# A projection with its weights stationary and 512 tokens moving, and its result brought to its partitions through DRAM

## The chip, the cores and the metric

The kernel runs on one core of a Trainium2 chip. The time is the device time of one execution in microseconds. Before the change it was 2569.82 us, the median of three runs (2568.74 to 2572.65).

Five engines work side by side, each through its own instructions in order: TensorE (PE; the loads of its stationary operand are listed apart, as PEld), VectorE (DVE), ScalarE (ACT), GpSimd (POOL) and SyncE (SP), which issues most of the DMAs. An instruction that waits holds back everything behind it on its engine.

## The reference

Two model blocks are computed one after the other for 1024 tokens of 1024 channels, in float32. The change touches the S5 branch of the first block alone:

```
z = x @ w_in                                    # x: 1024 tokens x 1024
u_a, v_a, g_a, x_b, g_b, q_x, g_x = split(z)    # x_b: 256 channels
# S5: 16 groups of 16 channels, 64 complex states each
bu = einsum('gpc,blgc->blgp', b_bar, x_b)
h  = scan over the tokens: h[l] = lam_bar * h[l-1] + bu[l]
y  = gelu(real(einsum('gcp,blgp->blgc', c, h)) + d * x_b)
y_b = y * sigmoid(y @ glu_w + glu_b)            # then times silu(g_b)
```

The other branches of the first block are a gated spatial mixing (u_a, v_a, g_a) and an attention over a memory of 256 tokens (q_x, g_x). Then follow `w_out`, a layer norm, and the second block: a recurrent branch, a differential attention, a second memory attention, and 32 experts of which each token takes two.

## The kernel before

**Products.** Every large product is made of three matmuls on operands in two parts (high and low, float32r), by `mm3` (lines 172 to 176): left high with right high, left low with right high, left high with right low. The left operand is the stationary one, the right one moves. x lies transposed in `xh` and `xl`: 128 channels on the partitions, eight such tiles, 1024 tokens along the row.

**S5 in chunks.** The tokens are cut into 128 chunks of `CT` = 8. Within a chunk the outputs are a matrix times the inputs; the states go from chunk to chunk by a scan. The branch needs x_b in an unusual shape, for each group of 16 channels a tile with place and channel (8 x 16 = 128) on the partitions and the 128 chunks along the row. Before the change this took two steps:

- `inputs` (lines 541 to 554): for each of the 8 places a product with x stationary (128 tokens, one of every eight, so a column every 32 bytes) and the 256 columns of `w_xb` moving. Over 8 places, 8 channel tiles and 3 parts these are 192 matmuls into the PSUM tile `pu`. ACT copies them to `U`: chunks on the partitions, place and channel along the row.
- in `s5`, once for each of four units u of four groups (lines 604 to 609): four transposes on TensorE into the PSUM tile `px`, then the split into the two parts `X`.

After it each unit computes `pst` (what a chunk adds to the states), turns and scans it on DVE and POOL, makes the states `h`, and computes `py` from `h` and from `X` with the matrix `K`. After two units the outputs are transposed (`pty`), copied to `Y`, and at the end `pz` is the product with `glu_w`.

**What sets the order.** `inputs` is issued at a high priority, before three lanes that `merge` (lines 71 to 118) puts side by side by clocks of their own: `left` (S5, then half of the gating), `attend` (memory attention, tiles `pk`, `pv`, `pq`, `sc`, `pt`, `po`, then the other half of the gating, again into `pv`), and `dense`, products of 512 tokens into the tile `pj` that fill in. A scheduler then fixes each engine's order when the program is built. The pools have few buffers, and some tags are shared: `xraw` (the raw tiles of x), `U`, `K` and `yt` take turns in the buffers u0, u1, k and yt; the high and low parts of chunked weights have two buffers each, which `w_xb` fills until `inputs` is through and into which `xa_w_k` goes then.

Of the kernel before, what the change touches and what calls it, by code (L numbers as in the profile page):

```python
# [28 lines left out]
BLK = 96                    # tokens of a block of an expert  # L29
NB = -(-1024 // BLK)        # blocks that one expert can have  # L30
NY = 3
N0 = 2                          # gated outputs of the first branch that go under the attention
CT = 8                          # tokens of a chunk of the S5 states
NRA, NRB, NRX = 6, 6, 1                 # buffers of the expert weights
OVAT = 8                        # expert beside which the further blocks are listed
LIM = 78                        # chunks of expert weights after which fewer buffers take them
EMPTY = 2048                    # the token of an empty row, beyond all
NOV = 2048 // BLK + 1       # more than the blocks beyond the first ones
# [32 lines left out]
def merge(tc, lanes, fill, made):  # L71
    """emits the lanes side by side: each moves its own clock on by its pace with every step, and the one
    that is behind comes next; the clock is the priority too. A lane yields None, a new place for its
    clock, the name of work of the last lane that it needs, or a condition that another lane will fulfil.
    The last lane only has products that fill in; what takes them out of PSUM, the functions that it
    yields, goes first."""
# [3 lines left out]
    late = []  # L80
# [49 lines left out]
class Model:  # L130
# [50 lines left out]
    def gelu2(self, out, ps, pool, shape, tag):  # L181
        """out = 2 * gelu(ps)"""
        q = pool.tile(shape, F32, name=tag + "q", tag=tag + "q")
        self.act(q, ps, AF.Square, scale=GC0)
        self.stt(q, q, 1.0, ps, OP.add, OP.mult)
        self.act(q, q, AF.Tanh, scale=GC1)
        self.stt(out, q, 1.0, ps, OP.add, OP.mult)

    def exp_small(self, out, x, pool, w, name):
        """accurate exp of a small tile [128, w]"""  # L190
# [24 lines left out]
    def sincos(self, s, c, r, pool, shape, name):  # L215
        """r in [-pi, pi]"""
        a = pool.tile(shape, F32, name=name + "a")
        self.act(s, r, AF.Sin)
        self.ts(a, r, -1.0, OP.mult)
        self.tt(a, a, r, OP.max)  # L220
        self.ts(a, a, -1.0, OP.mult, math.pi / 2, OP.add)
        return self.act(c, a, AF.Sin)
# [14 lines left out]
    # ------------------------------------------------------------------  # L237
    def setup(self):
# [13 lines left out]
        # half biases for sigmoids made of tanh  # L252
# [4 lines left out]
        # residents that live into the second block  # L257
# [5 lines left out]
    def params(self, P):  # L263
        """S5 and rope tables, softplus of the LRU parameter, lambda of the differential attention;
        yields between its steps"""
# [8 lines left out]
        # S5: step, lambda * step  # L274
# [14 lines left out]
        # rotation of one step and of its doublings, up to half of all tokens  # L289
# [17 lines left out]
        # expm1(a) = 2 tanh(a/2) / (1 - tanh(a/2))  # L307
# [11 lines left out]
        # lambda to the powers 0 .. CT, and what a chunk leaves of a state's modulus  # L319
# [4 lines left out]
        for lev in range(4):  # L324
# [5 lines left out]
            if 0 < lev < 3:  # L330
                # the powers up to n times this one
# [11 lines left out]
        # f = (lambda_bar - 1) / lambda  # L343
# [13 lines left out]
        # b_bar = f * b  # L357
# [11 lines left out]
    def params2(self, P):  # L369
        nc, A = self.nc, self.A  # L370
        t = lambda k, w=8: P.tile([128, w], F32, name="par2_" + k)
        # rope angles
# [12 lines left out]
        # softplus(-lambda) of the LRU  # L385
# [19 lines left out]
        # lambda of the differential attention  # L405
# [11 lines left out]
    def s5_tables(self, x, y, tb, u):  # L417
        """cos(CT theta c), sin(CT theta c) of the chunks c, of two state tiles"""
# [16 lines left out]
        # ends with the last doubling  # L435

    # ------------------------------------------------------------------
    # first block
    # ------------------------------------------------------------------
# [12 lines left out]
    def block1(self):  # L452
# [29 lines left out]
        # x transposed, in two parts  # L482
# [13 lines left out]
        def group(ps, ws, h):  # L496
            """one product of 512 tokens, whole"""
# [27 lines left out]
        def store_y(k, t0, y, n):  # L525
            """n token tiles of channel tile k"""
# [3 lines left out]

        # ---- S5, in chunks of CT tokens: token CT c + t is place t of chunk c. Within a chunk the outputs
        # are a matrix times the inputs; the states go from chunk to chunk ----
        U = [S5.tile([128, 8, CT, 16], F32, name="U", tag=f"u{ct}") for ct in range(2)]
        # matrices with blocks of zeros that stay: states to outputs, inputs to states
# [6 lines left out]
        def inputs():  # L541
            """x_b with the chunks on the partitions; the places backwards"""
            for m in range(CT // 2):
                ps = PB.tile([128, 2, 256], F32, name="pu", tag="pb", bufs=2)
                for s in range(2):
                    t = 2 * m + 1 - s
                    for k in range(8):
                        w = w_xb[k // 4]
                        v = [z[:, k].rearrange("p (c t) -> p t c", t=CT)[:, t] for z in (xh, xl)]
                        self.mm3(ps[:, s], v, (w[0][:, k % 4], w[1][:, k % 4]), k == 0, k == 7)  # L550
                for ct in range(2):
                    j = CT - 2 - 2 * m
                    self.act(U[ct][:, :, j:j + 2].rearrange("p g j c -> p j g c"),
                             ps[:, :, 128 * ct:128 * ct + 128].rearrange("p s (g c) -> p s g c", c=16), AF.Copy)

        def s5():
            yield from self.params2(P)
            parp.__exit__(None, None, None)
            for u in range(4):
# [6 lines left out]
                def times(m, n, sign):  # L566
                    """m lambda^k, k < n; sign is that of the second part of m"""
# [13 lines left out]
                # states to outputs: c lambda^k  # L581
# [5 lines left out]
                # inputs to outputs: c lambda^k b, k < CT, with zeros before; every place's row is a window of it  # L587
# [16 lines left out]
                # inputs, places and channels on the partitions  # L604
                pb = PB.tile([128, 4, 128], F32, name="px", tag="pb", bufs=2)
                for g in range(4):
                    nc.tensor.transpose(pb[:, g], U[ct][:, 4 * (u % 2) + g].rearrange("p j c -> p (j c)"), self.ident)
                X = [S5.tile([128, 4, 128], F32R, name="xg", tag=f"xg{k}") for k in "hl"]
                self.split(X[0], X[1], pb)
                yield  # L610
                # what a chunk adds to the states
# [15 lines left out]
                # turned back, the states decay by a real factor  # L627
# [22 lines left out]
                # the states before each chunk  # L650
# [14 lines left out]
                # 2 gelu  # L665
# [12 lines left out]
                if u % 2:  # L678
                    # back to channels on the partitions
# [8 lines left out]
            # y_b = y * sigmoid(glu) * silu(g_b); y comes doubled  # L688
# [131 lines left out]
        def gating(hp, side, wload, vps, pm_):  # L820
            """two heads of the gating; wload loads weights, vps and pm_ say where in PSUM"""
# [1624 lines left out]
```

## Time and profile before

| | us |
|---|---|
| median of three runs | 2569.82 |
| span of the profiled execution, first to last instruction | 2566.8 |
| median less span (what lies around the span; the profile prints no time of its own for it) | 3.0 |
| TensorE busy in the span | 2402.1 |
| VectorE busy in the span | 1774.3 |
| `inputs`, starts of the first and the last matmul | 37.1 and 87.4 |
| start of the last `pty` of S5 | 304.1 |

A matmul's listed duration is not the time it adds: matmuls overlap, and where they follow one another without a gap the distance from start to start counts. Slices and stretches in which PE is busy throughout are those in which it had always something to do. The granted clock is 1 at 2.4 GHz and 0.5 at 1.2 GHz; a mean between the two says how much of a stretch had which.

### The profile page before, as it was taken

The page shows a single profiled execution, that of the slowest core. Times are in us where ns is not written, and L with a number is a line of the kernel's source. Part 1 is how long each engine was busy: PE and PEld are TensorE (multiplying, and loading weights), DVE is VectorE, ACT ScalarE, POOL GpSimd, SP SyncE. Part 2 cuts the span into 40 slices and gives each one's busy share as a digit, 9 for nine tenths or more (in the row PEclk, how much of TensorE's full clock was granted, in tenths as well). Part 3 has the DMA queues.
Part 4 walks back from the last instruction along what each step waited for, and adds up shares of the span by engine and source line. Part 5 has one row for each costly group of instructions (what it writes and reads, how often), then busy time and mean ns, then how long its engine had stood idle before and what let it go on. Part 6 is the DMA issues. An engine that isn't in the chain of part 4 may idle for free. (4 is left out here: it accounts for less than half of the span.)

```text
span 2566.8 us, 34716 instructions
## 1 busy us (share of the span) xinstructions
PE 2402.1 (94%) x13128; PEld 1993.8 (78%) x13128; DVE 1774.3 (69%) x3153; ACT 1246.6 (49%) x1854; POOL 595.1 (23%) x425
## 2 busy tenths in 40 slices
PE   6999989999999999999999989999998998999997
PEld 5988877777788889889898778888876776766665
DVE  8367576777796666666665654334557998998897
ACT  4234532344565445445445532124435776776665
POOL 4312212312222121121021010001222332233343
PEclk9999999999999999999999999999998999999999
DMA  4221245412221111101101256642246997999995
GB/s 167 63 73 63 81 140 173 134 68 78 72 85 46 50 42 54 54 30 54 61 35 40 92 193 211 200 154 91 83 197 243 366 379 284 331 372 359 353 341 200
DMA packets 101688, 392.18 MB, mean 153 GB/s; under 512 B 14352, under 2 KB 31248, under 8 KB 76944
## 3 DMA queue, kind: packets, MB, share of 16 engines
q1 hardware_dynamic: 82992, 333.31, 36.0%
q0 software_dynamic: 18528, 56.65, 7.0%
q8 instruction: 104, 1.70, 0.3%
q14 instruction: 64, 0.52, 0.1%
HBM read 338.02 MB, written 60.26 MB: 155 GB/s over the span
## 5 line engine op out<-in xcount | busy, mean ns | idle before, releaser
L154 ACT ACTIVATE wh<-raw 128x2048 fp32r<-128x2048 f32 (+2 forms) x310 | 480.0, 1557 | 322.4 <-PE pj L175 84.4
L166 DVE TENSOR_TENSOR wl<-raw,wh 128x2048 fp32r<-128x2048 f32 (+2 forms) x287 | 553.5, 1939 | 94.4 <-ACT wh L154 93.9
L174 PE MATMUL pj<-wh,xnh 128*128 128x256 f32 x768 | 222.9, 290 | 9.0 <-ACT pc L154 4.8
L2214 POOL DMA_INDIRECT out<-y,lsti x32 | 146.8, 4588 | 355.6 <-DVE y L162 351.2
L176 PE MATMUL pj<-wh,xnl 128*128 128x256 f32 x768 | 218.4, 284 | 0.0
L175 PE MATMUL pj<-wl,xnh 128*128 128x256 f32 x768 | 217.9, 284 | 0.0
L175 PE MATMUL pg<-wl,xh 128*96 128x512 f32 x512 | 205.1, 401 | 13.3 <-DVE wl L166 12.6
L176 PE MATMUL pg<-wh,xl 128*96 128x512 f32 x512 | 201.9, 395 | 0.0
L174 PE MATMUL pg<-wh,xh 128*96 128x512 f32 x512 | 200.5, 397 | 0.0
L174 PEld LDWEIGHTS pj<-wh,xnh 128*128 128x128 f32 x768 | 145.7, 190 | 11.9 <-ACT pc L154 6.7
L179 POOL TENSOR_TENSOR ss<-ss,mhalf 128x4 f32<-128x4 f32 (+1 forms) x68 | 74.3, 1093 | 315.5 <-DVE ss L163 223.5
L175 PEld LDWEIGHTS pj<-wl,xnh 128*128 128x128 f32 x768 | 146.6, 191 | 0.0
L176 PEld LDWEIGHTS pj<-wh,xnl 128*128 128x128 f32 x768 | 145.6, 190 | 0.0
L154 ACT ACTIVATE e<-sc,st,ss 128x1024 f32<-128x1024 f32 (+7 forms) x128 | 105.6, 828 | 67.8 <-DVE st L158 50.5
L175 PEld LDWEIGHTS pg<-wl,xh 128*96 128x96 f32 x512 | 82.8, 162 | 55.8 <-DVE wl L166 23.2
L174 PEld LDWEIGHTS pg<-wh,xh 128*96 128x96 f32 x512 | 83.0, 162 | 37.3 <-ACT wh L154 2.2
L176 PEld LDWEIGHTS pg<-wh,xl 128*96 128x96 f32 x512 | 83.2, 162 | 33.3 <-DVE xl L166 0.2
L174 PE MATMUL pj<-xnh,wh 128*128 128x512 f32 x256 | 103.3, 404 | 5.6 <-ACT wh L154 5.6
L174 PE MATMUL pg<-xnh,wh 128*128 128x512 f32 x256 | 103.7, 405 | 0.0
L175 PE MATMUL pg<-xnl,wh 128*128 128x512 f32 x256 | 102.6, 401 | 0.0
L176 PE MATMUL pg<-xnh,wl 128*128 128x512 f32 x256 | 102.4, 400 | 0.0
L175 PE MATMUL pj<-xnl,wh 128*128 128x512 f32 x256 | 102.2, 400 | 0.0
(1001 smaller groups left out, 6673.1 us busy)
## 6 DMA issues: line engine op xcount, KB each, us to landing
raw<-in_w_gu SPq DMA_DIRECT2D x128, 1024.0 KB, 8.7
raw<-in_w_dn SPq DMA_DIRECT2D x64, 1024.0 KB, 9.6
raw<-in_w_out SPq DMA_DIRECT2D x16, 512.0 KB, 4.0
ta<-tg POOLq DMA_DIRECT2D x32, 256.0 KB, 2.7
t<-ta SPq DMA_DIRECT2D x14, 512.0 KB, 4.7
raw<-in_w_ga SPq DMA_DIRECT2D x12, 512.0 KB, 3.7
raw<-in_w_v SPq DMA_DIRECT2D x12, 512.0 KB, 3.5
xraw<-in_xT SPq DMA_DIRECT2D x8, 512.0 KB, 6.9
```

The costliest lines, as they stand in the source:

```text
L154: return self.nc.scalar.activation(out=out, in_=in_, func=func, **kw)
L166: return (eng or self.nc.vector).tensor_tensor(out=out, in0=a, in1=b, op=op)
L174: mm(ps, l[0], r[0], start=start, stop=False)
L175: mm(ps, l[0], r[1], start=False, stop=False)
L176: mm(ps, l[1], r[0], start=False, stop=stop)
L179: self.nc.gpsimd.tensor_tensor(out=out, in0=in_, in1=self.mhalf[:, :w], op=OP.pow)
L2214: return nc.gpsimd.indirect_dma_start(out=self.out, out_offset=bass.IndirectOffsetOnAxis(ap=u["row"], axis=0), in_=u["y"], in_offset=None, ...
```

## The change

`inputs` now runs over two channel tiles ct and two halves h of the tokens. The 128 columns of `w_xb` are stationary and 512 neighbouring tokens move, as in `dense`: 2 x 2 x 8 x 3 = 96 matmuls of 512 columns. ACT copies each result into the tile `xbt` with places and chunks in another order. `xbt` is stored to DRAM (`xbd`, 512 KB for each ct), and eight DMAs for each ct (64 KB each, runs of 512 bytes) load it so that place and channel are on the partitions: `U` now has the shape that the transposes made. The 16 transposes are gone; `X` is split from `U` in SBUF. `xbt` takes the buffers k and yt.

```diff
-        U = [S5.tile([128, 8, CT, 16], F32, name="U", tag=f"u{ct}") for ct in range(2)]
+        U = [S5.tile([128, 8, 128], F32, name="U", tag=f"u{ct}") for ct in range(2)]
+        xbd = [D.tile([128, CT, 128], F32, name=f"xbd{ct}") for ct in range(2)]
...
-            for m in range(CT // 2):
-                ps = PB.tile([128, 2, 256], F32, name="pu", tag="pb", bufs=2)
-                for s in range(2):
-                    t = 2 * m + 1 - s
+            for ct in range(2):
+                xt = S5.tile([128, CT, 128], F32, name="xbt", tag=("k", "yt")[ct])
+                for h in range(2):
+                    ps = PB.tile([128, 512], F32, name="pu", tag="pb", bufs=2)
                     for k in range(8):
-                        w = w_xb[k // 4]
-                        v = [z[:, k].rearrange("p (c t) -> p t c", t=CT)[:, t] for z in (xh, xl)]
-                        self.mm3(ps[:, s], v, (w[0][:, k % 4], w[1][:, k % 4]), k == 0, k == 7)
-                for ct in range(2):
-                    j = CT - 2 - 2 * m
-                    self.act(U[ct][:, :, j:j + 2].rearrange("p g j c -> p j g c"),
-                             ps[:, :, 128 * ct:128 * ct + 128].rearrange("p s (g c) -> p s g c", c=16), AF.Copy)
+                        w = [z[:, k % 4, 128 * ct:128 * ct + 128] for z in w_xb[k // 4]]
+                        self.mm3(ps, w, (xh[:, k, hs(h)], xl[:, k, hs(h)]), k == 0, k == 7)
+                    self.act(xt[:, :, 64 * h:64 * h + 64], ps.rearrange("p (c t) -> p t c", t=CT), AF.Copy)
+                nc.sync.dma_start(out=xbd[ct], in_=xt)
+                for j in range(CT):
+                    nc.sync.dma_start(out=U[ct][16 * j:16 * j + 16],
+                                      in_=xbd[ct][:, CT - 1 - j].rearrange("(g i) c -> i g c", i=16))
...
-                pb = PB.tile([128, 4, 128], F32, name="px", tag="pb", bufs=2)
-                for g in range(4):
-                    nc.tensor.transpose(pb[:, g], U[ct][:, 4 * (u % 2) + g].rearrange("p j c -> p (j c)"), self.ident)
                 X = [S5.tile([128, 4, 128], F32R, name="xg", tag=f"xg{k}") for k in "hl"]
-                self.split(X[0], X[1], pb)
+                q = 4 * (u % 2)
+                self.split(X[0], X[1], U[ct][:, q:q + 4])
```

The order of the instructions moves with it. On PE, at the end of `inputs`, there stood before (`pu` is the product of `inputs`, `pm` the first product of S5):

```order
L174 MATMUL pu<-wh,xh 128x256
L175 MATMUL pu<-wl,xh 128x256
L176 MATMUL pu<-wh,xl 128x256
L174 MATMUL pm<-Gh,bbh 16x256
L175 MATMUL pm<-Gl,bbh 16x256
L176 MATMUL pm<-Gh,bbl 16x256
```

and now stands

```order
L174 MATMUL pu<-xh,wh 128x512
L175 MATMUL pu<-xl,wh 128x512
L176 MATMUL pu<-xh,wl 128x512
L174 MATMUL pm<-Gh,bbh 16x256
L175 MATMUL pm<-Gl,bbh 16x256
L176 MATMUL pm<-Gh,bbl 16x256
```

The row ahead of `pm` is the same in kind, but half as many matmuls of twice the columns lie there, and five more `pj` stand among them. (The names after the arrow are read moving operand first, then stationary.)

On ACT, in the same place, this piece of the difference shows the copies (`U` before, `xbt` now), the splits of S5 (`Gh`, `xg`) and the split of the weights `xa_w_k` (`wh`):

```order
-L154 ACTIVATE U<-pu 128x2x8x16 x3
+L154 ACTIVATE xbt<-pu 128x8x64
 L154 ACTIVATE bbh<-bbar 128x256
-L154 ACTIVATE U<-pu 128x2x8x16 x3
-L154 ACTIVATE wh<-raw 128x1024
-L154 ACTIVATE U<-pu 128x2x8x16 x2
-L154 ACTIVATE wh<-raw 128x1024
+L154 ACTIVATE xbt<-pu 128x8x64
+L154 ACTIVATE Gh<-gf 64x4x144 x2
+L154 ACTIVATE xbt<-pu 128x8x64
+L154 ACTIVATE xg<-U 128x512
+L154 ACTIVATE wh<-raw 128x1024 x2
+L154 ACTIVATE xbt<-pu 128x8x64
```

`xg<-U`, which needs the eight loads from DRAM, now stands ahead of both `wh` and of the last copy; `Gh`, which stood far ahead, comes after the store of the first `xbt`, whose buffer (k) its source `gf` takes.

On PE at the tail of S5 there stood before (`pt` are transposes of the memory attention, `pj` is the filling work of `dense`):

```order
L684 MATMUL pty<-ident,yt 128x128 x8
L803 MATMUL pt<-ident,e 128x128 x2
L174 MATMUL pj<-xh,wh 128x512
...
L175 MATMUL pj<-xl,wh 128x512
L174 MATMUL pz<-yh,glh 128x512
L175 MATMUL pz<-yl,glh 128x512
```

and now stands

```order
L683 MATMUL pty<-ident,yt 128x128 x8
L174 MATMUL pj<-xh,wh 128x512
L175 MATMUL pj<-xl,wh 128x512
L176 MATMUL pj<-xh,wl 128x512
L802 MATMUL pt<-ident,e 128x128 x4
L174 MATMUL pz<-yh,glh 128x512 x2
L175 MATMUL pz<-yl,glh 128x512
```

Before, 23 `pj` stood between `pty` and the first `pz` that needs its result; now there are 3, and the other 20 stand earlier. From the layer norm on, the order of PE is the same in both but for some twenty rows of the attention.

## Rows read from the trace of the kernel before

**Rows 1.** The page: busy time of each engine, share of the span, instructions.

```profile
PE 2402.1 (94%) x13128; PEld 1993.8 (78%) x13128; DVE 1774.3 (69%) x3153; ACT 1246.6 (49%) x1854; POOL 595.1 (23%) x425
```

**Rows 2.** Busy time by stretch: us, each engine (instructions), granted clock, DMA share, GB/s.

```profile
40.00:90.00 50.00, 50.00 (x217) 49.03 (x217) 20.07 (x107) 12.07 (x22) 5.51 (x3) 1.00 0.17 55
...
120.00:130.00 10.00, 7.00 (x43) 5.95 (x42) 9.88 (x10) 4.46 (x6) 9.88 (x5) 1.00 0.01 2
130.00:140.00 10.00, 8.16 (x35) 7.48 (x36) 7.79 (x46) 0.28 (x1) 0.20 (x1) 0.66 0.60 197
...
200.00:300.00 100.00, 98.42 (x559) 84.24 (x558) 67.01 (x181) 48.95 (x108) 29.19 (x18) 1.00 0.22 69
...
330.00:390.00 60.00, 47.84 (x348) 44.15 (x348) 46.35 (x170) 24.96 (x57) 12.07 (x18) 0.91 0.36 122
```

**Rows 3.** The tile pu: durations in ns (min/median/max), first and last start.

```profile
L174 PEld LDWEIGHTS pu<-wh,xh x64: 334/337/341, 36.7 to 86.8; 128*128 128x128 f32 x64
...
L176 PE MATMUL pu<-wh,xl x64: 398/404/408, 38.8 to 87.4; 128*128 128x256 f32 x64
```

**Rows 4.** Timeline of TensorE: start, length; first and last of 44 pu in a row.

```profile
49.13 0.41 PE L175 MATMUL pu<-wl,xh 128*128 128x256 f32 x1
...
59.51 0.40 PE L174 MATMUL pu<-wh,xh 128*128 128x256 f32 x1
```

**Rows 5.** Timeline of TensorE: 24 pj in a row, the first and what follows the last.

```profile
249.59 0.40 PE L174 MATMUL pj<-xh,wh 128*128 128x512 f32 x1
...
255.06 0.39 PE L174 MATMUL sc<-kph,qh 128*128 128x512 f32 x1
```

**Rows 6.** The tile pv, x of 128 neighbouring tokens stationary: durations in ns.

```profile
L174 PEld LDWEIGHTS pv<-wh,xh x128: 186/192/193, 263.8 to 375.3; 128*128 128x128 f32 x128
```

**Rows 7.** Timeline of TensorE: 256-column pv, the first and last of 8.

```profile
123.79 0.28 PE L175 MATMUL pv<-wl,mh 128*128 128x256 f32 x1
...
124.63 0.28 PE L176 MATMUL pv<-wh,ml 128*128 128x256 f32 x1
```

**Rows 8.** Timeline of TensorE: four transposes px, and what follows them.

```profile
209.12 0.60 PE L607 MATMUL px<-ident,U 128*128 128x128 f32 x4
209.48 0.48 PE L174 MATMUL sc<-kph,qh 128*128 128x512 f32 x1
209.79 0.40 PE L175 MATMUL sc<-kpl,qh 128*128 128x512 f32 x1
```

**Rows 9.** Timeline of TensorE: where py waits for the states of the first tile.

```profile
131.84 0.58 PE L176 MATMUL py<-Gh,h 128*128 128x256 f32 x1 [4.84 <-DVE h L166]
```

**Rows 10.** Timeline of TensorE: the tail of the S5 branch.

```profile
304.11 1.03 PE L684 MATMUL pty<-ident,yt 128*128 128x128 f32 x8
...
310.71 0.39 PE L174 MATMUL pz<-yh,glh 128*128 128x512 f32 x1
...
318.23 0.80 PE L175 MATMUL pz<-yl,glh 128*128 128x512 f32 x1 [2.31 <-DVE yl L166]
```

**Rows 11.** Timeline of ScalarE: from the last transposes to the split.

```profile
306.39 2.20 ACT L154 ACTIVATE Y<-pty 128x512 f32<-128x512 f32 x2
...
309.69 0.64 ACT L154 ACTIVATE yh<-Y 128x512 fp32r<-128x512 f32 x1
```

**Rows 12.** Timeline of VectorE: the other half of that split.

```profile
310.37 0.69 DVE L166 TENSOR_TENSOR yl<-Y,yh 128x512 fp32r<-128x512 f32 x1 [0.61 <-ACT yh L154]
```

**Rows 13.** Timeline of SyncE's queue: one store to DRAM and the eight loads from it.

```profile
91.67 0.69 SPq L599 DMA_DIRECT2D kd<-mk  x1
...
94.19 5.09 SPq L602 DMA_DIRECT2D K<-kd  x8
```

**Rows 14.** The tile K: its loads, us from issue to landing (min/median/max).

```profile
DMA to landing us min/median/max: 2.5/2.6/3.9
```

**Rows 15.** DMA issues up to 330 us: KB each, median us to landing.

```profile
atb<-du SPq DMA_DIRECT2D x8, 256.0 KB, 2.0
...
raw<-in_xa_w_k SPq DMA_DIRECT2D x2, 512.0 KB, 4.2
```

## The prediction

> **What bounds the kernel now.** I read the page first: TensorE is busy for 2402.1 of 2566.8 us [rows 1], so work taken off it is worth its time unless another engine is late there. Then the stretches [rows 2]: from 40 to 90 us, which is `inputs` with some `pj`, PE is busy in all 50 us at full clock while DVE has 20 and ACT 12 us of work. That stretch is PE's alone. It stays so up to 300 us (98.42 of 100 us from 200 to 300, DVE 67), with one hole, between 120 and 140 us, at a granted clock of 0.66 behind it. From 330 to 390 us it is shared: PE 47.84 of 60 us, DVE 46.35. So I expect a saving in `inputs` to be carried through S5 and to be questioned first at its tail.
>
> Then the tile `pu`. Its weight load takes 337 ns [rows 3]. 43 steps from the first to the last start of a run without a gap take 10.38 us, 0.2414 us each [rows 4]. The same kind of load for the gating, x of 128 neighbouring tokens, takes 192 ns [rows 6], and 256-column matmuls behind such loads step by 0.84/7 = 0.120 us [rows 7]. So it is the load of every eighth token that sets the step of `pu`, twice what its columns need. A 512-column `pj`, which has `inputs`' new form (same moving x, weights of 128 neighbouring columns stationary), steps by 5.47/24 = 0.228 us [rows 5].
>
> The Trainium skill, "TensorE: Matmul & The Clock Gate", sections "Back-to-back issue gap" and "LDWEIGHTS (loading the stationary operand)", speaks against this change: the gap is the columns over 2.4 GHz plus some 2.5 ns, and a load depends on its columns alone (128 of them, about 107 ns). By it 192 matmuls of 256 columns and 96 of 512 cost the same, 20.9 and 20.7 us, an estimate from that page of the Trainium skill, and term 1 below would be nothing. This trace agrees for `pj` (0.228 against 0.216) and for contiguous loads (0.120 against 0.109), not for `pu`.
>
> **The change, part by part.**
>
> 1. The products. Removed 192 x 0.2414 = 46.3 us, added 96 x 0.228 = 21.9 us: -24.4 us. No DMA is due in this stretch that PE would outrun: the weights and x are in SBUF before it (`pu` runs from 38.7 us, a step before the 38.8 of [rows 3], to 87.4 + 0.24 = 87.6, without a gap [rows 2]).
>
> 2. The transposes. Four of them take 0.36 us until the next matmul starts, which then steps by 0.31 instead of about 0.23 [rows 8]. Sixteen: 4 x 0.36 = 1.4 us, up to 4 x 0.44 = 1.8. I take -1.5 us.
>
> 3. The copies and splits. Four copies instead of eight, and a split that reads SBUF instead of PSUM, on ACT and DVE, which have 38 and 30 us free of 50 there [rows 2]. Nothing, while PE covers it.
>
> 4. The way through DRAM. The trace has no 512 KB store; 256 KB stores land after 2.0 us and 512 KB loads after 4.2 us [rows 15], so 2 to 5 us; I take 4, nearer to the row of the same size. The eight loads are like those of `K`: issues over 5.09 us [rows 13], the last landing 2.6 us (at most 3.9) later [rows 14]. Together 4 + 5.1 + 2.6 = 11.7 us. In PE's new order 44 of the 48 matmuls of ct 0 and 8 `pj` stand from 38.7 us on (4 before): the end is 38.7 + 52 x 0.228 = 50.6 us, the last copy is made by about 52, so `U` for ct 0 is there at 63.7 us. With the 48 of ct 1 and 12 more `pj`, `inputs` ends at 38.7 + 112 x 0.228 = 64.2 us, 23.4 us before the old end, with five more `pj` (1.1 us) done by then. So `xg<-U` on ACT is ready just when PE comes to `pm`. Behind it in ACT's queue stand both `wh` of `xa_w_k` and the last copy; behind them `pk` on PE. `gf`, on DVE, waits for the store (its buffer k) until 56 us, which leaves 8 us for its way to `pm`. Each microsecond that the loads are later than 64 is paid by PE. I take +0.5 us; bounds 0 and +5 (the largest landing, 3.9, and a store as slow again as a load). On SP the second ct's eight loads stand ahead of `K`'s: 5.1 us more for `K`, which is used over 20 us later, by the order. `w_qx` behind it has the same cover.
>
> 5. The hole at 127 us. `py` of the first unit waits 4.84 us for `h` [rows 9], which DVE delivers late; after it the clock is 0.66 for 10 us [rows 2], 6.8 us at 1.2 GHz, of which 5 lie behind the wait: 2.5 us lost. In the new order 22 `pj` instead of 8 stand between the last `pv` and this `py`: 14 x 0.228 = 3.2 us more cover. The wait falls to 1.6 us if DVE and POOL are as slow; POOL's order now has a weight split between two of that chain's steps, so it might be longer. I take -3.2 for the wait and -0.8 of the 2.5 for the clock: -4. Bounds 0 and -7.3.
>
> 6. The tail of S5. The filling work is finite: what stands earlier is missing later. After the last `pty`, 23 `pj` cover the way `pty`, `Y`, `yh`, `yl` to `pz`: from 305.1 us (`pty`'s end) to 311.1 (`yl`'s end) [rows 10 to 12], 5.9 us, and the first `pz` has no wait. Now 3 `pj` and four transposes are left, 1.1 us. ACT's queue has a weight split, a copy of a `pj` result and two exponentials between `Y` and `yh`, much as before, so the way stays near 6 us: 4.8 us of new wait, and I add 0.6 for a weight split ACT may wait for: +5.4. The second half's wait of 2.31 us [rows 10] loses the cover of 12 `po` (1.4 us): +1.1. A clock that falls, as behind the hole: +0.5 of up to 2.5. Together +7, bounds 0 (if scheduling leaves the chain ahead) and +10.
>
> Behind that the gating has PE and DVE almost equally full; its waits are on work that moves with it, and PE's order from the layer norm on is the same. I cost it at nothing, with +-2 us for where the clock falls.
>
> Sum: -24.4 - 1.5 + 0.5 - 4 + 7 = -22.4 us. On the profiled span: 2566.8 - 22.4 = 2544.4; with the 3.0 us that lie between span and median, 2547.4 us. I say 2547. The change is to be told from none at 0.2%, 5 us.
>
> **Rivals.**
>
> a) Full gain (0.12). Nothing new waits at the tail, and the hole goes with its clock loss: -24.4 - 1.5 - 7.3 = -33 us, 2537. For it: DVE and ACT have room in rows 2. Against it: 20 `pj` fewer at the tail.
>
> b) The tail takes more (0.20). Each of the four units is bound by its own chain, and the filling work, being done early, hides less: +10 at the tail, +5 at the loads, the hole unchanged: -24.4 - 1.5 + 15 = -11 us, 2559. For it: the hole shows that such a chain can be late by 5 us when PE outruns it. Against it: units 2 to 4 show no such hole in 200 to 300 us.
>
> c) No gain (0.04). Columns alone set the time, or the strided reading costs on the moving side what it did on the stationary one: term 1 is nothing, -1.5 + 0.5 - 4 + 7 = +2, 2572. Against it: `pu` and `pj` step as they do in the same stretch. The rule of the Trainium skill cited above would give this.
>
> d) Slower (0.03). ACT is held by `xg<-U`. Its place is between `inputs` and `pk`; its price is a microsecond for each that the loads of ct 0 land after 64 us. It makes the kernel slower from 64 + 22 = 86 us on, 34 us behind the copy: three times the 11.7 us above. At 45 us behind it, 2580. Against it: `kd` to `K`, the same way with a smaller store, takes 94.19 + 5.09 + 2.6 - 91.67 = 10.2 us [rows 13, 14].
>
> **The numbers.** The forecast, with 2541 to 2554 as its own range, has 0.61; a) to d) as given. The range that holds 8 in 10 reaches to both neighbours: 2537 to 2560. Faster by over 0.2%: 0.91, all of the forecast, a) and nearly all of b); within 0.2%: 0.06, c) and what b) loses; slower: 0.03, d).
>
> **What would show it.** Right: `pu` at 96 matmuls of 512 columns with a load near 190 ns and a step of 0.228; the first `pm` at 64 to 66 us instead of 87.6; no `px`; the last `pty` some 21 us earlier, as 20 `pj` (4.6 us) have gone ahead of it; a wait of 4 to 6 us of `pz` on `yl`; the hole before the first `py` shorter than 2 us. Wrong: a gap on PE between `inputs` and `pk` whose releaser is ACT or a DMA (term 4); a step of `pu` near 0.24 or above (term 1); a wait of `py` in units 2 to 4, or a gating whose waits grow by what came early (term 6).

## The result and the profile after the change

The changed kernel took 2541.1 us (median of four runs, 2537.9 to 2542.3), the kernel before beside it 2570.8 (four runs, 2568.7 to 2572.7): a ratio of 0.9879, with a 95% interval of 0.9868 to 0.9891. It is faster by 30 us, where 23 were forecast. Eight later runs of the same kernel, two medians of 2535.6 and 2537.7, gave ratios of 0.9867 [0.9852, 0.9882] and 0.9875 [0.9859, 0.9892]; over all twelve runs the median is 2537.9. So the time lies far nearer to rival a (2537) than to the forecast (2547).

The profiled execution has a span of 2540.4 us, 26.4 less than before. Its page, in the columns of [rows 1]:

```profile
PE 2381.8 (94%) x13016; PEld 1966.0 (77%) x13016; DVE 1775.6 (70%) x3153; ACT 1245.3 (49%) x1850; POOL 594.0 (23%) x425
```

TensorE has 20.3 us less to do; the other engines have what they had. The share of busy time is the same 94%, which says nothing on where the time went. For that, the program is cut at five instructions whose order is the same in both kernels, and the starts are read from the timeline of TensorE. Us of each stage, and the differences from before, with the prediction's terms put into the same stages (20 `pj`, 4.6 us, that move from behind the last `pty` to ahead of it are in both columns):

| stage | before | predicted | after | its second profile | its third |
|---|---|---|---|---|---|
| to the first `pj` that waits for the last `xl` | 34.4 | 0 | -2.1 | -3.1 | -2.2 |
| `inputs`, to the first `pm` | 53.2 | -23.3 | -23.0 | -23.2 | -22.8 |
| the units of S5, to the last `pty` | 216.5 | -1.6 | -0.2 | -0.3 | -0.1 |
| tail of S5, to the gating's first `pv` | 18.7 | +2.5 | -2.8 | -2.8 | -4.2 |
| gating, to the layer norm's first `ptr` | 114.2 | 0 | -0.6 | -3.8 | -2.8 |
| everything else | 2129.8 | 0 | +2.4 | -1.8 | -1.1 |
| span | 2566.8 | -22.4 | -26.4 | -34.9 | -33.2 |

The large term is right; the first stage and the tail are not. The rows that answer to those shown before:

The tile `pu` and its stream on TensorE (durations in ns as in [rows 3]; then the first and what follows the last of 48 in a row, start and length in us, as in [rows 4]):

```profile
L174 PEld LDWEIGHTS pu<-xh,wh x32: 187/188/330, 34.6 to 61.6; 128*128 128x128 f32 x32
...
L176 PE MATMUL pu<-xh,wl x32: 388/389/395, 37.1 to 62.3; 128*128 128x512 f32 x32
```

```profile
51.61 0.39 PE L174 MATMUL pu<-xh,wh 128*128 128x512 f32 x1
...
62.48 0.28 PE L174 MATMUL pm<-Gh,bbh 128*16 128x256 f32 x1
```

The load takes 188 ns instead of 337, and the step is 10.87/48 = 0.226 us. No gap stands between the last `pu` and `pm`.

The way through DRAM, on SyncE's queue, then on ScalarE, then the landing of the loads:

```profile
52.88 0.33 SPq L553 DMA_DIRECT2D xbd<-xbt  x1
55.50 3.66 SPq L555 DMA_DIRECT2D U<-xbd  x8
```

```profile
61.36 0.63 ACT L154 ACTIVATE xg<-U 128x512 fp32r<-128x512 f32 x1 [2.14 <-DMA U<-xbd]
61.90 1.99 ACT L154 ACTIVATE wh<-raw 128x1024 fp32r<-128x1024 f32 x2
```

```profile
DMA to landing us min/median/max: 2.3/2.6/3.5
```

The store is through after 2.6 us, not 4, and the eight issues take 3.7 us, not 5.1. ScalarE waits 2.1 us, TensorE not at all.

The hole ahead of the first `py`, and the granted clock around it (columns as in [rows 9] and [rows 2]):

```profile
102.01 0.50 PE L174 MATMUL pj<-xh,wh 128*128 128x512 f32 x1 [0.60 <-DVE du L158]
...
106.66 0.39 PE L176 MATMUL py<-Gh,h 128*128 128x256 f32 x1 [2.07 <-DVE h L166]
```

```profile
100.00:110.00 10.00, 7.21 (x29) 5.33 (x27) 9.66 (x42) 1.07 (x3) 3.60 (x2) 0.86 0.47 144
110.00:120.00 10.00, 10.00 (x52) 8.54 (x51) 5.66 (x19) 2.35 (x4) 0.00 (x0) 0.97 0.24 80
```

4.84 us of waiting [rows 9] became 0.60 + 2.07, and the clock falls less.

The tail of S5 on TensorE, to be held against [rows 10]:

```profile
278.77 1.03 PE L683 MATMUL pty<-ident,yt 128*128 128x128 f32 x8
...
281.61 0.50 PE L174 MATMUL pz<-yh,glh 128*128 128x512 f32 x1 [0.43 <-ACT Y L154]
...
284.33 0.97 PE L174 MATMUL pz<-yh,glh 128*128 128x512 f32 x2 [1.29 <-ACT yh L154]
...
286.32 0.79 PE L175 MATMUL pz<-yl,glh 128*128 128x512 f32 x1 [1.02 <-DVE yl L166]
```

The waits are 2.74 us together, hardly more than the 2.31 of [rows 10], though the cover of 20 `pj` is gone. The last of them is for `yl`, on VectorE:

```profile
284.40 1.87 DVE L166 TENSOR_TENSOR yl<-Y,yh 128x512 fp32r<-128x512 f32 x1
```

The clock differs here between profiles of the one kernel. The stage from the last `pty` to the gating's first `pv`, in the first profile and in the third:

```profile
278.77:294.60 15.83, 13.09 (x56) 9.50 (x55) 9.99 (x16) 9.75 (x18) 4.04 (x2) 0.78 0.33 98
```

```profile
279.02:293.47 14.45, 10.77 (x56) 7.99 (x55) 9.85 (x15) 9.67 (x19) 4.06 (x2) 1.00 0.29 93
```

The granted clock was 0.78 in the first (and in the second) and 1.00 in the third, whose waits are 3.7 us and whose stage is 1.4 us shorter all the same.

In the last stage this execution gave 2.4 us back, and its two later profiles did not. One stretch shows part of the reason: behind a wait of the same length (2.55 us of `pj` on `wh` in both) the granted clock was 0.91 in the one and 1.00 in the other. The changed kernel in its first profile, then in its second:

```profile
611.00:631.00 20.00, 15.36 (x94) 13.73 (x94) 13.66 (x11) 16.13 (x20) 3.71 (x2) 0.91 0.24 76
```

```profile
604.50:624.50 20.00, 15.32 (x101) 13.43 (x100) 13.83 (x11) 16.03 (x20) 3.80 (x3) 1.00 0.24 81
```

The same busy time held 94 matmuls at the lower clock and 101 at the full one. Which of the two comes is a matter of the single execution, not of the change: both profiles are of the same kernel.

### The profile page after: what moved, and what is told of

It is laid out like the page before. It is cut to its first block, busy times and chain, and to the rows that moved or that the text cites. A ratio compares the mean times of both kernels' runs of the same rounds, so it can differ in the third digit from the quotient of the medians.

```text
span 2540.4 us, 34497 instructions
## 1 busy us (share of the span) xinstructions
PE 2381.8 (94%) x13016; PEld 1966.0 (77%) x13016; DVE 1775.6 (70%) x3153; ACT 1245.3 (49%) x1850; POOL 594.0 (23%) x425
## 5 line engine op out<-in xcount | busy, mean ns | idle before, releaser
L175 PEld LDWEIGHTS pg<-wl,xh 128*96 128x96 f32 x512 | 82.8, 162 | 55.8 <-DVE wl L166 23.2
L176 PE MATMUL pj<-xnh,wl 128*128 128x512 f32 x256 | 102.4, 401 | 0.0
```

What stands on the lines that cost most here:

```text
L175: mm(ps, l[0], r[1], start=False, stop=False)
L176: mm(ps, l[1], r[0], start=False, stop=stop)
```

## The experiments

**Only the stride of the stationary operand (near).** The kernel before, its order of instructions unaltered on every engine.

```diff
-                        v = [z[:, k].rearrange("p (c t) -> p t c", t=CT)[:, t] for z in (xh, xl)]
+                        v = [z[:, k, 128 * t:128 * t + 128] for z in (xh, xl)]
```

> The kernel before, with one thing altered: the stationary x of pu is 128 neighbouring tokens (128 t to 128 t + 127) instead of every eighth one, so the places get other tokens than they should. The 192 matmuls of 256 columns, the copies, the transposes and the order of every engine stay. Theory (the load of every eighth token sets the step): the load falls from 337 to about 190 ns, the step from 0.241 to 0.120 us, so 192 x 0.121 = 23 us go: the first pm starts at about 64.5 us instead of 87.6, and the whole takes 2544 to 2550 us. Rival (half as many matmuls of twice the columns is what counts): step and time stay, 2568 to 2573. Rival (most of the gain is the order and the transposes): load and step fall, but less than 10 us of it reaches the end.

2547.9 us (five runs), ratio 0.9912 [0.9899, 0.9926]: 23.2 us less than before. Its tile `pu`:

```profile
L176 PEld LDWEIGHTS pu<-wh,xl x64: 187/192/192, 38.2 to 64.2; 128*128 128x128 f32 x64
L176 PE MATMUL pu<-wh,xl x64: 279/283/283, 38.4 to 64.3; 128*128 128x256 f32 x64
```

192 matmuls of 256 columns step by 0.120 us; the first `pm` starts at 64.45 us, and of the 23.2 us that it is earlier 20.7 are left in the span and 23.2 in the medians. So nearly the whole of the products' term comes from reading x without a stride; what the number and size of the matmuls add is 192 x 0.120 - 96 x 0.226 = 1.3 us at most. The hole is as long as before, to the hundredth, only 23 us earlier:

```profile
108.70 0.58 PE L176 MATMUL py<-Gh,h 128*128 128x256 f32 x1 [4.84 <-DVE h L166]
```

**The stride on the moving side (eighth, second).** The changed kernel with x moving at a stride; the output places of a copy change with it, so that the result stays.

```diff
-                        self.mm3(ps, w, (xh[:, k, hs(h)], xl[:, k, hs(h)]), k == 0, k == 7)
+                        v = [z[:, k].rearrange("p (c t) -> p t c", t=CT)[:, 4 * h:4 * h + 4] for z in (xh, xl)]   # eighth
+                        v = [z[:, k].rearrange("p (n s) -> p s n", s=2)[:, h] for z in (xh, xl)]                  # second
...
```

(The product with `v` and the copy to `xbt` are left out here.)

> The changed kernel, but the moving x of pu is read at every eighth token: four places of 128 chunks, 32 bytes from one column to the next, instead of 512 neighbouring tokens. What is computed stays; the copy to xbt writes in order. Theory (a stride costs on the stationary side alone): step of pu 0.228 us, no difference, 2538 to 2544. Rival c of the prediction (the stride costs on the moving side what it did on the stationary one): the step doubles to about 0.45 us, 96 x 0.22 = 21 us more, 2558 to 2566.

> The changed kernel, but the moving x of pu is every second token (512 tokens, 8 bytes from one column to the next); what is computed stays. With every eighth token moving the step of pu was 0.436 us instead of 0.228 and the whole 2557 us. Theory (any step between columns costs twice): step 0.43 us again, 21 us more than the changed kernel, 2555 to 2560. Rival (it is the distance of 32 bytes that costs): step 0.228, 2535 to 2542. Between the two: a cost that grows with the distance, a step of 0.25 to 0.4.

2557.0 us for every eighth token (ratio 0.9944 [0.9930, 0.9957]) and 2557.0 for every second (0.9956 [0.9941, 0.9970]), 19 us above the changed kernel's 2537.9. Here 48 `pu` in a row, the first and what follows the last, of every eighth token, then of every second:

```profile
60.92 0.59 PE L174 MATMUL pu<-xh,wh 128*128 128x512 f32 x1
...
81.60 0.30 PE L174 MATMUL pm<-Gh,bbh 128*16 128x256 f32 x1
```

```profile
62.20 0.61 PE L174 MATMUL pu<-xh,wh 128*128 128x512 f32 x1
...
83.94 0.30 PE L174 MATMUL pm<-Gh,bbh 128*16 128x256 f32 x1
```

The steps are 20.68/48 = 0.431 and 21.74/48 = 0.453 us, about twice the 0.226 without a stride, with a granted clock of 1.00 in all three stretches. My theory that only the stationary side pays fell; what rival c's second half says of the moving side came true, and the change escapes it because its 512 moving tokens are neighbours. The distance hardly matters: 8 bytes cost as much as 32, or a little more. The Trainium skill, "SBUF — State Buffer", section "Door 1: The DMA port swizzle (why `[64,N]` ≈ `[32,N]`)", says that a read pays when it goes to a new line of 16 bytes and that two reads of each line suffice for the full rate, which a step of 8 bytes still gives. The 32-byte rows agree with it, the 8-byte rows (0.453 us) do not, and the measurement decides.

**The way through DRAM made longer (detour).** Three copies from DRAM to DRAM between store and loads.

```diff
-                nc.sync.dma_start(out=xbd[ct], in_=xt)
+                z = [nc.sync.dma_start(out=xbd[ct][n], in_=xbd[ct][n - 1] if n else xt) for n in range(4)]
...
```

(The loads of `U`, left out here, read the last of the four.)

> The changed kernel, but x_b goes through three more copies from DRAM to DRAM (512 KB each) between its store and the loads of U, one behind the other. Each takes about what the store took, 2.6 us, to what a load of that size takes, 4.2 us (plus its issue): U of the first half is there 8 to 14 us later, at 69 to 75 us. Theory (rival d of the prediction with its point right behind the end of inputs): ACT sits in xg<-U, behind it the two wh, behind them pk on PE: slack of about 1 us, then every microsecond is paid: a gap of 7 to 13 us on PE ahead of pk, the whole 5 to 13 us longer, 2546 to 2554. Rival (pj and pst's late place cover it, as U is first multiplied at 75 us): no gap on PE, 2538 to 2544.

2545.3 us, ratio 0.9898 [0.9882, 0.9913]; the changed kernel beside it 2535.6: 9.7 us more. ScalarE's order had changed: both `wh` went ahead of `xg`, so `pk` was not late. The wait moved to the first product that needs U (ScalarE, then TensorE):

```profile
74.25 0.63 ACT L154 ACTIVATE xg<-U 128x512 fp32r<-128x512 f32 x1 [7.59 <-DMA U<-xbd]
78.25 1.06 ACT L154 ACTIVATE wh<-raw 128x1024 fp32r<-128x1024 f32 x1 [3.37 <-DMA raw<-in_xa_w_v]
...
79.47 0.26 ACT L154 ACTIVATE Bh<-pbt 128x128 fp32r<-128x128 f32 x1
```

```profile
79.78 0.33 PE L174 MATMUL pst<-xg,Bh 128*128 128x128 f32 x1 [3.87 <-ACT Bh L154]
```

`pst` waits for `Bh`, which stands on ScalarE behind `xg` and behind a split of `xa_w_v`, and SyncE issued the load of `xa_w_v` (72.84 us) only after those of U. U was 12.9 us later than in the changed kernel, 10 us behind the 64 us from which the prediction let each microsecond count. The place I named, `pk`, was wrong, and the wait is 3.87 us, not 7 to 13. Behind it the clock fell. Here are the same matmuls, from this `pst` on, in detour and then in the second profile of the changed kernel:

```profile
79.78:83.72 3.94, 3.89 (x17) 3.53 (x18) 1.84 (x5) 2.09 (x4) 3.93 (x2) 0.62 0.24 61
```

```profile
74.26:76.35 2.09, 2.09 (x18) 2.04 (x17) 0.20 (x1) 0.00 (x0) 1.46 (x1) 1.00 0.46 110
```

They took 1.9 us more. So 10 us of lateness cost 5.7 us at this place, less than a microsecond for each: TensorE had other products until 75.9 us. TensorE is then 7.4 us behind that second profile, of which 1.5 were there by 37 us; where the rest of the 9.7 came from stays open.

**Transposes put back, four times as many (sixteen).**

```diff
+                z = [nc.tensor.transpose(pb[:, g % 4], U[ct][:, q + g % 4], self.ident) for g in range(16)]
...
```

> The changed kernel, with 16 transposes of U for each unit put back on PE (64 in all, four times as many as the change took away; nothing reads their result). Theory (a transpose costs 0.09 us of PE's stream, as the four px in 0.36 us before the change): 64 x 0.09 = 5.8 us longer than the changed kernel measured beside it. Rival (they lie in waits that PE has anyway, and their removal gave nothing): within 1.5 us. Rival (each costs more, by the weight load of the transpose ahead and the step behind it, up to 0.11 each): 7 us.

2544.9 us against 2537.7 beside it, 7.2 us more, 0.11 for each of the 64 if all of it is theirs. The ends alone do not show that: the order moved with them, 48 `pj` stand behind the last `pty` instead of 3, and TensorE's waits moved from the tail (none is left) into S5 (8.4 us instead of 3.7). The stream itself shows the price. Sixteen in a row, and what follows them:

```profile
80.06 1.91 PE L607 MATMUL px<-ident,U 128*128 128x128 f32 x16
81.72 0.48 PE L174 MATMUL pj<-xh,wh 128*128 128x512 f32 x1
82.04 0.40 PE L175 MATMUL pj<-xl,wh 128*128 128x512 f32 x1
```

They take 1.66 us, and the step behind them is 0.32 instead of 0.23: 0.10 to 0.11 us each. So the dearer transpose fits, and the change's 16 were worth 1.4 [rows 8] to 1.8 us of TensorE's stream, as term 2 had it.

**The tail without its own cover (pzlast).** The second channel tile first.

```diff
-                    for k in range(2):
-                        self.mm3(pz, ..., k == 0, k == 1)
+                    for k in (1, 0):
+                        self.mm3(pz, ..., k == 1, k == 0)
```

> The changed kernel, but pz takes the second channel tile first, whose outputs are those of the last pty, and the first tile's last. Theory (term 6 of the prediction was too large because the first six pz need only the first tile, whose outputs were long there, and stand as cover between pty and what needs its result): the cover of 6 x 0.23 = 1.4 us is gone, pz waits 3 to 5 us at the start instead of 0.4 + 1.3 + 1.0, and the stretch from the last pty to the gating's first pv (15.8 us) is 1 to 3 us longer. Rival (the way pty, Y, yh, yl is itself short enough): the stretch stays within 0.5 us.

2542.9 us, ratio 0.9891 [0.9876, 0.9905], 5 us above 2537.9. The tail on TensorE:

```profile
280.31 1.04 PE L683 MATMUL pty<-ident,yt 128*128 128x128 f32 x8
...
285.83 0.73 PE L174 MATMUL pz<-yh,glh 128*128 128x512 f32 x2 [3.35 <-ACT yh L154]
...
287.83 0.79 PE L175 MATMUL pz<-yl,glh 128*128 128x512 f32 x1 [1.26 <-DVE yl L166]
```

From the last `pty` to the gating's first `pv` it takes 18.3 us at a granted clock of 0.81; the changed kernel takes 15.8 in the two profiles whose clock was as low (0.78) and 14.4 in the third (1.00). So the six `pz` of the first channel tile, whose inputs are long there, are cover worth 2.5 us at a like clock. The other 2.5 us of the total are not of this stage, and no run explains them.

**Who is late at the head (xbdve, alldve, xdve).** First two weights, then all chunked weights of the first block are split by DVE instead of POOL; the third variant adds to the first the two x tiles that POOL splits.

```diff
-            w_xb = [chw(A["w_xb"][j], [128, 4, 256]) for j in range(2)]
+            w_xb = [weights(A["w_xb"][j], [128, 4, 256], "c", eng=None) for j in range(2)]      # xbdve
-        chw = lambda src, shape=[128, 8, 128]: weights(src, shape, "c")
+        chw = lambda src, shape=[128, 8, 128]: weights(src, shape, "c", eng=None)               # alldve
-                self.split(xh[:, k], xl[:, k], raw, nc.gpsimd if k % 3 == 2 else None)
+                self.split(xh[:, k], xl[:, k], raw)                                             # xdve
```

> The changed kernel, but the low parts of the two w_xb chunks are made by DVE instead of POOL. Theory (a DVE instruction that runs beside a weight split of POOL lasts as long as what is left of it, 2.3 us instead of 0.15, and the last xl stands behind them): two such stretched instructions go (-4.4 us), two splits of 1.2 us come if they stand ahead of the last xl, so the first pj behind xl starts 2 to 4 us earlier than in the two profiles of the changed kernel (32.3 and 31.4), at 28 to 30 us, and the whole gains 1 to 4 us over it. Rival (the stretched instructions follow from DVE's own work or the table loads): xl is not earlier, or later by 2 us, the whole 0 to 2 us longer.

> The changed kernel, but the low parts of all chunked weights of the first block (w_xb, xa_w_k, xa_w_v, w_qx) are made by DVE instead of POOL. Theory (the hole before the first py is DVE's chain stretched beside POOL's weight splits: hu and gf 2.6 us each instead of 0.4): these take 0.4 us, the waits of 0.6 and 2.1 us before py shrink to under 1.5 together, and the head gains as in the kernel with w_xb alone; 2 to 6 us less than the changed kernel. Rival (DVE, at 71% of its time between 175 and 275 us, becomes late with some 10 more splits of 1.2 us): py waits as long or longer, the whole 0 to 5 us longer.

> As the kernel whose w_xb is split by DVE (2529.8 us beside 2569.8 of before), and the two x tiles that POOL still split go to DVE too: no POOL split stands beside DVE's chain ahead of the last xl but the one of w_gb. Theory (each POOL split costs a DVE instruction 2.3 us, a split on DVE 1.2): up to 2 x 1.1 us less, the first pj behind xl at 28 to 29 us instead of 30.1, the whole 0 to 2 us shorter, 2527 to 2530. Rival (DVE is late for the early xl now, as it has eight of them): 0 to 3 us longer.

> The kernel with the low parts of w_xb made by DVE once more, to settle whether it is faster than the changed kernel, whose twelve runs lie between 2533.8 and 2542.3 us with a median of 2537.9. Theory (two instructions of DVE's chain ahead of the last xl are no longer stretched, and what that gives at the head reaches the end): 2529 to 2534 us again, xl at 29 to 30.5 us. Rival (its first five runs were lucky, and the head start is given back at the tail of S5, as in the kernel whose x is split by DVE alone): 2536 to 2542.

2529.8 us (0.9850 [0.9838, 0.9863]) for the first, and 2532.9 (0.9857 [0.9841, 0.9874]) when run again: a median of 2532.6 over nine runs, 5.3 below the changed kernel's, of which only two of twelve runs reach into its range. 2530.7 (0.9849 [0.9837, 0.9862]) for all weights. 2540.2 (0.9878 [0.9861, 0.9894]) with x as well, beside 2537.7 for the changed kernel.

The rows that set it up. VectorE before the change; two of four instructions on 128x8 tiles that take 2.3 us, where their like take 0.16; GpSimd at the same time:

```profile
24.80 2.31 DVE L166 TENSOR_TENSOR C<-C,par_w 128x8 f32<-128x8 f32 x1
27.11 2.31 DVE L158 SCALAR_TENSOR_TENSOR par_nr<-par_sh,par_nr 128x8 f32<-128x8 f32 x1
```

```profile
20.05 2.37 POOL L166 TENSOR_TENSOR xl<-xraw,xh 128x1024 fp32r<-128x1024 f32 x1 [5.02 <-DMA xraw<-in_xT]
22.37 7.02 POOL L166 TENSOR_TENSOR wl<-raw,wh 128x1024 fp32r<-128x1024 f32 x3
```

After the change POOL has two `wl` there, VectorE three stretched instructions, and the last `xl` comes 2.1 us earlier:

```profile
22.38 2.40 POOL L166 TENSOR_TENSOR wl<-raw,wh 128x1024 fp32r<-128x1024 f32 x1
24.99 2.36 POOL L166 TENSOR_TENSOR wl<-raw,wh 128x1024 fp32r<-128x1024 f32 x1 [0.22 <-ACT wh L154]
```

In the first variant POOL has one, VectorE two, and the first `pj` behind `xl` starts at 30.1 us in both of its profiles (the changed kernel: 32.3, 31.4, 32.2; with all weights on DVE 28.8). The theory holds for these. The hole stayed in the first variant, as 4.14 us at the `pq` behind the first `py`, and shrank to 0.98 us there in the second; their times are the same, so closing it brought nothing that shows at the end. Of the first variant's 5.3 us the head shows some 2. The order moved too: 16 `pj` stand behind the last `pty` instead of 3, and `pz` waits 0.95 us there instead of 2.7 to 3.7. No run parts the two.

With x split by DVE too that `pj` starts at 25.8 us, 6.4 earlier than in the changed kernel beside it, and the end is 2.5 us later. Waits further on, on TensorE, took part of that time:

```profile
97.89 0.39 PE L176 MATMUL py<-Gh,h 128*128 128x256 f32 x1 [4.28 <-DVE h L166]
```

```profile
280.78 0.80 PE L174 MATMUL pz<-yh,glh 128*128 128x512 f32 x1 [3.69 <-ACT Y L154]
```

```profile
PE pm L174 <- ACT vh L154: 6.3, 1, 6.3
PE po L174 <- ACT yh L154: 4.5, 1, 4.5
PE prs L839 <- ACT wsh L154: 2.5, 1, 2.5
```

(The last fence is TensorE's waits in the gating: us in total, times, longest.) From the first `pm` to the last `pty` the waits are 7.5 us, against 3.7 in the changed kernel beside it; in the gating 16.7 against 14.9; at the tail 3.8 against 3.7, so the one `pz` wait is no loss. In S5 that fits rival b's mechanism, work done early that leaves chains uncovered, brought on by another edit. The gating took 115.5 us there and 111.4 beside it, but its granted clock was 0.91 against 0.95, and 5.2 of the 7.5 us between the two spans lie behind the gating, where profiles of one kernel differ by 4.2. So the waits do not account for the whole loss.

**The changed kernel again (again, again2).** Unaltered.

> The changed kernel, unaltered, for a second profile and more times. Theory: 2538 to 2543 us; the waits of py (2.1 us) and pz (0.4, 1.3 and 1.0) come again, and the 2.8 us that were given back at two places of the second block (behind waits of the same length as before, with a lower granted clock) are a matter of the single execution: the clock falls there in one profile and not in another. Rival: they are lost at the same two places again, and belong to the change.

> The changed kernel once more, beside these two on one chip, so that the three can be compared. The changed kernel had 2541.1 us in its first four runs and 2535.6 in the next four, on another chip: 2535 to 2542 expected, and the waits of pz, py and xl as in its two profiles.

2535.6 and 2537.7 us. The first `py` waits 2.07 us in both; `pz` waits 0.43, 1.29 and 0.93 us in the one and 0.43, 1.29 and 1.25, with 0.71 further on, in the other. The stretch of the second block with a clock of 0.91 had 1.00 in the second profile, as shown above.

## Why the prediction was right, and where it was not

Term 1 (products, -24.4 us). Right in cause and size. `inputs` is 23.0 us shorter with five more `pj` (1.1 us) in it, which makes 24.1; the kernel near alone, with the stride gone and all else kept, gives 23.2.

Term 2 (transposes, -1.5). Right for TensorE's stream: -1.4 to -1.8, by [rows 8] and the 0.10 to 0.11 us of sixteen. What their removal alone gives at the end no run shows.

Term 3 (copies, 0). Right: nothing waits for `xbt` on TensorE.

Term 4 (DRAM, +0.5). It was 0: ScalarE had U at 61.4 us, not 63.7. The store began at 52.9 us instead of 52, but it and the issues were quicker by 2.8 us. The cover is what the prediction said or more. The price behind it was too high: detour's U came 10 us behind the 64 us and cost 5.7 us there, at `pst` and not at `pk`.

Term 5 (hole, -4). From the first `pm` to the last `pty` the stage is 0.2 us shorter with 16 more `pj` (3.6 us) in it: 3.9 together; without 1.5 to 1.8 for the transposes some 2.2 us are left, the 4.84 - 0.60 - 2.07 = 2.2 that these waits gave. Nothing is left over for the clock, though it fell less (0.86 and 0.97, against 0.66 in [rows 2]); what took that back is not shown. Inside its bounds, but half its value.

Term 6 (tail, +7). This is the step that failed. The stage has 21 `pj` fewer (4.8 us) and is 2.8 us shorter, so the tail cost 2.0 us (0.6 in the third profile, at the full clock). The prediction, like the section on the change, took the 3 `pj` and four transposes for all that stands between the last `pty` and the first `pz` that needs it. In fact six `pz` stand there too, which need the first channel tile alone, before as after; pzlast takes them away, and the tail then costs 2.5 us more. The way itself was not shorter than forecast: from the end of `pty` (279.80 us) to the end of the `yl` shown above (286.27) it took 6.5 us, against 5.9 before. The second part of the term failed as well: the later wait of 2.31 us was to grow by 1.1, and it is gone in two profiles and 0.71 in the third. So the sign that was named, a wait of 4 to 6 us of `pz` on `yl`, did not come: those waits are 0.9 to 1.3 us. (The text's "some 21 us earlier" for the last `pty` was also a slip: its own terms give 29.4 - 4.6 = 24.8, and 25.3 were measured.)

Not foreseen: the head, -2.1 to -3.1 us. The change frees no work there, but one weight split left POOL's order ahead of the last `xl`, and VectorE's chain is shorter by one stretched instruction. The kernel near, with the old order, has its `pj` at 33.4 us and before at 34.4, the changed kernel at 31.4 to 32.3; so one to two of these microseconds go with the order of the changed kernel, and the rest with the single execution.

The gating, costed at 0 within 2, came 0.6 to 3.8 us shorter. Between the three profiles of the changed kernel it goes with the granted clock: 113.6, 110.4 and 111.4 us at 0.92, 0.97 and 0.95, with 14 to 15 us of waits in each. Before it was 114.2 us at 0.94, with 16 us of waits. So most of the spread is the clock of the single execution; what part of the rest is the change's stays open.

So the forecast gain of 22.4 us becomes about 31 when the tail's 5 and the head's 2 to 3 are put right, the gating's 1 to 4 and the 0.5 of term 4 are added, and the hole's missing 1.8 are taken off. The three spans are 26.4, 34.9 and 33.2 us shorter. That the forecast came as near as it did is in part luck: the errors of terms 5 and 6 had opposite signs. The median of all twelve runs, 2537.9, lies outside its own range (2541 to 2554), and inside the range that holds 8 in 10 by 1 us. Rival a gave the number, but not for its reasons: hardly anything new waits at the tail, as it said, while the hole gave 2.2 us and not 7.3, and the head and the gating, which it does not name, made up for that.

## What to carry to other kernels

Look at the load and the step of a matmul's operands for each shape apart: a stride between the columns of a float32r operand about doubled the step here, on the stationary side at 32 bytes and on the moving side at 32 and at 8, and rearranging the result through DRAM was free under other products. Before costing a wait at a moved consumer, look which of its instructions need the late result and which can stand ahead of it. Time gained early need not reach the end: the edit that gave 5 us for two weights gave nothing for two weights and two tiles of x, with new waits in S5 where the fill-in work had gone ahead. And before a difference of a few microseconds between two profiles is put down to an edit, compare the granted clock of the stage, in several profiles of one kernel.

## What the runs showed of the hardware

- Operands at a stride: 0.241 us for 256 columns behind a strided load and 0.120 without; 0.431 (32 bytes) and 0.453 us (8 bytes) for 512 strided moving columns and 0.226 without.
- An elementwise VectorE instruction on a 128x8 tile beside a GpSimd split lasted until that split ended: 2.31 to 2.36 us instead of 0.16, one for each split of 2.4 us. The Trainium skill, "SBUF — State Buffer", section "SBUF: two separate sides", describes the port pair that the two engines share as an exclusive lock held for a whole instruction; these rows agree, and a split on VectorE (1.21 us) was then cheaper for the chain behind it than the same split on GpSimd beside it.
- A 512 KB copy from DRAM to DRAM took about 4 us from one to the next for the first channel tile (three between 55.85 and the first load of `U` at 67.89 us). A 512 KB store from SBUF landed after 2.6 us for the first tile and after 5.1 for the second, so the 2.6 is not a general price.
- Behind waits of about the same length the granted clock was 0.91 in one profile and 1.00 in another of one kernel, and a stage that took 15.8 us at 0.78 took 14.4 at 1.00.
